# A planner's TensorE costs from measured spacings, another order of the projections, and buffers kept for the last heads

## The chip, the cores and the metric

The kernel runs on one core of a Trainium2 chip. The metric is the device time of one execution in microseconds (us), as the median of several runs. A core has TensorE (PE: matrix products and transposes, with its weight loads as PEld), VectorE (DVE), ScalarE (ACT), GpSimd (POOL) and SyncE (SP), which issues the DMAs here. Each engine takes its instructions in the order in which the program lists them, and waits for the results that an instruction needs.

## The reference

Two layers work on 512 tokens of width 1024. Each layer has one input projection whose columns feed three mixers side by side, one output projection, a norm, and an MLP with a hidden layer of 4096.

```python
for l in range(DEPTH):
    proj = h @ w_in[l]
    ...
    mixed = concatenate([nsa_mixer(nq, nkv, ngate, ...),      # 6 query heads, 2 kv heads
                         gla_mixer(gq, gk, gv, glr, gog, ...), # 6 heads, chunks of 64
                         pool_mixer(pu, pool_w[l], pool_scale[l])])
    h = layer_norm(ALPHA * h + mixed @ w_out[l], ln1_g[l], ln1_b[l])
    ff = square(relu(h @ w_up[l])) @ w_down[l]
    h = layer_norm(ALPHA * h + ff, ln2_g[l], ln2_b[l])
```

The attention mixer (`nsa_mixer`) rotates queries and keys (partial rotary embedding), and mixes three branches by gates: keys compressed from blocks of 32 tokens by a small two-layer network, selected blocks, and a window. The gated linear attention (`gla_mixer`) computes a masked product inside each chunk of 64 tokens, a running state over the chunks, a norm of each head and an output gate. All is float32.

## The kernel before

Float32 products are made of three products of parts: each operand is split into a rounded high part and a remainder (type float32r), ACT makes the high part and VectorE or GpSimd subtracts to get the low part. Weights arrive by DMA in units of up to 512 KB, in a fixed order, four raw units at a time; each unit is split the same way (`splits`, L342 on), and the unit's products may run when the split is done.

What sets the order on every engine is a planner (`class Planner`, L35 to L126), which runs while the program is built. Each piece of work is a generator, and has a priority; a `yield` ends a step and names what the next step waits for: events, a free PSUM bank (of 8), or a free slot among the NSLOT = 46 buffers of 128 x 512 floats. Whenever a piece of work is ready by the planner's own clock, its next step is emitted; when none is, a step of the background is, which is the weight products. The planner's clock is advanced by estimates: `MM` (L174) and `TR` (L180) carry those of TensorE, `act`, `tt`, `ts`, `stt`, `red` (L185 to L220) those of the others. `tt` with the engine "any" takes VectorE or GpSimd, by which of the two would end sooner by the estimates (L197 to L200).

The background of a layer runs through blocks in the order of the letters in `ORDER` (L1662): A values of the gated linear attention, B its queries and keys, D the first keys and values of the attention (K0, V0, K1: features as rows, 512 tokens as columns), E its other values and the gates (tokens as rows, 274 columns), F the keys K2, W the first layer of the network for compressed keys, G the queries, C the input of the trailing means, O the output gate, P and R those rows of the output projection that do not need the attention, N its other three rows. After that comes the MLP. Its first six tiles of rows of `w_up` are held in slots once they are split (`held`, L303 and L362) and used by `early_up` (L1317), each for the first 256 tokens as soon as those are normed, and for the others later; `out_rest` of tokens 256 to 511 stands between the first two tiles' products and the others'.

Around that background stand, as generators of their own:

- `states` (L697 on) and `intra` (L733 on), small products of the gated linear attention with 32 or 64 rows, `intra_mask` (L761, a mask on VectorE), and then for each tile of 128 tokens 28 small products or fewer with 64 columns and the states, and `rms` (L769);
- `rope` (L891): a shuffle on VectorE (L893) out of PSUM, two multiplications and a sum; K0 and V0 are then arranged by `im2col` (L955);
- `attention` (L1097), which starts one `head` (L1106) after another, first for tokens 0 to 255 (H = 0), six heads in two branches each, then for tokens 256 to 511 (H = 1). A head's products fill PSUM; VectorE takes the maximum, ACT the exponential, VectorE or another engine scales, TensorE transposes, ACT and VectorE split, TensorE multiplies with the values. The pair of heads 2m, 2m + 1 makes row m of the output projection's operand (`nmix`), by ACT, VectorE, ACT, VectorE.

Of the kernel before, what the change touches and what calls it, by code (L numbers as in the profile page):

```python
# [9 lines left out]
F32 = mybir.dt.float32  # L10
F32R = mybir.dt.float32r
# [23 lines left out]
class Planner:  # L35
    """Fixes the order in which each engine gets its instructions.

    A piece of work is a generator.  It emits instructions, and a yield ends a step: None waits for what the step
    has emitted, a list waits for conditions (names of events, or ("bank", n) for n free PSUM banks).  The matrix
    products of the projections are the background; they fill the tensor engine between the steps of the others.  # L40
    """
# [61 lines left out]
    def run(self):  # L103
        back_cond = None
        while self.work or self.back is not None:
            ready = [w for w in self.work if self.when(w[3]) <= self.now]
            if ready:
                w = min(ready, key=lambda w: w[:2])
                more, cond = self.step(w[2])
                if more:  # L110
                    w[3] = cond
                else:
                    self.work.remove(w)
                continue
            if self.back is not None and self.when(back_cond) <= self.now:
                more, cond = self.step(self.back)
                back_cond = cond if isinstance(cond, list) else None
                if not more:
                    self.back = None
                continue  # L120
            times = [self.when(w[3]) for w in self.work]
            if self.back is not None:
                times.append(self.when(back_cond))
            t = min(times)
            assert t < math.inf, ("nothing can go on", [w[3] for w in self.work], back_cond)
            self.now = max(self.now, t)  # L126
# [3 lines left out]
def trunk_kernel(ctx: ExitStack, tc, x, w_in, cmp_pos, cmp_w1, cmp_w2, gla_w_gate2, gla_b_gate,  # L130
# [12 lines left out]
    pl = Planner()  # L143
# [7 lines left out]
    def drop(n=1):  # L151
        """n slots have got their last reader"""
        pl.live -= n
# [20 lines left out]
    def MM(o, a, b, start, stop, loose=False):  # L174
        n = b.free_size()
        pl.pe(max(0.025, n / 2400.0 * (4 if b.dtype == F32 else 1) + 0.0025))
        nc.tensor.matmul(o, a, b, start=start, stop=stop, **({"skip_group_check": True} if loose else {}))  # L177
        pl.ready[o.tensor.name] = pl.now + 0.2

    def TR(o, a, i):  # L180
        pl.pe(0.056)
        nc.tensor.transpose(o, a, i)  # L182
        pl.ready[o.tensor.name] = pl.now + 0.2
# [157 lines left out]

    def splits():  # L342
# [14 lines left out]
        for i in range(len(units)):  # L357
# [4 lines left out]
            if i in held:  # L362
                yield [("raw", i), ("h", held[i] + 0.5, 0), ("slot", 1)]
                hi, lo = [slot(dt=F32R).rearrange("p (k n) -> p k n", k=kk) for _ in range(2)]
            else:
                yield [("raw", i)] + room(i)
                hi = wp.tile([128, kk, n], F32R, tag="whi", name=f"wh{i}", bufs=NSPL)
                lo = wp.tile([128, kk, n], F32R, tag="wlo", name=f"wl{i}", bufs=NSPL)
# [4 lines left out]
    def pair_sums(i0, i1, room, order):  # L373
        """operands of the seven products (Winograd's form of Strassen's) for two tiles of rows of the hidden layer"""
# [88 lines left out]
    def transpose_h(l, t, hT):  # L463
        """(l, t): tokens t of the input of layer l, or of its MLP for l + 0.5"""
# [50 lines left out]
    def passes(ps, sh, sl_, mh, ml, first, last, loose=False):  # L515
        """three products of parts: stationary (sh, sl_), moving (mh, ml)"""
# [35 lines left out]
    def layer_work(l, hT, nhT):  # L552
# [264 lines left out]
        def mixed(ks, t):  # L817
            """what the products with rows ks of w_out need for tile t"""
# [218 lines left out]
        def cmp_tile(t):  # L1037
            """probabilities of the compressed branch for one tile of queries"""
# [58 lines left out]
        def attention():  # L1097
            for H in range(2):
                for hh in range(6):
                    for br in (1, 2):  # L1100
# [3 lines left out]
                        pl.spawn(head(H, hh, br), 4)  # L1104

# [211 lines left out]
        def early_up(m, H, ffp, acc):  # L1317
            """rows m of the first part of the MLP's hidden layer, for half H of the tokens"""
# [24 lines left out]
        def token_sums():  # L1343
            """sums and differences of quarters (half of the rows, half of the tokens) of the MLP's input"""
# [43 lines left out]
        def up_pairs(up, ff):  # L1388
            """the hidden layer, two tiles of rows at a time; the last two products of a pair come among the next's"""
# [11 lines left out]
        def up_pair(i0, i1, ff, m):  # L1401
            """two tiles of rows of the hidden layer by seven products of quarters"""
# [259 lines left out]
ORDER = 'ABDEFWGCOPNR'  # L1662
# [59 lines left out]
```

## Time and profile before

| | |
|---|---|
| three runs | 1256.07, 1264.20, 1262.56 us (median 1262.56) |
| the profiled execution, its span | 1255.8 us |
| busy TensorE (PE) | 1232.5 us, 98%, 7377 products |
| busy VectorE (DVE) | 914.2 us, 73% |
| busy ScalarE (ACT) | 589.8 us, 47% |
| busy GpSimd (POOL) | 288.3 us, 23% |

The profiled execution's own time is its span; what lies around it is not in the profile, and the lowest of the runs is 0.3 us above it. Busy time of TensorE is modelled from the ends of products, so small gaps inside a run of products do not show as idle time; starts of products do show them. Layer 1 takes the first 630 us or so, and layer 2 repeats its stretches; times below are of layer 1.

### The profile page before, as it was taken

To read this page: it belongs to the slowest core of one execution; us is meant where nothing else is said; L and a number is where in the kernel's file an instruction comes from. 1 tells how busy PE (TensorE), PEld (TensorE's weight loads), DVE (VectorE), ACT (ScalarE), POOL (GpSimd) and SP (SyncE) were. 2 spreads that over 40 slices of the span, in tenths; PEclk is the share of its full clock that TensorE was granted. 3 is DMA by queue.
4 is the path that set the end of the run, shared out by engine and by line. 5 is a ranking of instruction groups with operands and counts; after the bars stand their busy time and mean duration, and the time that the engine had idled before them with its cause. 6 is when DMAs were issued, how large, how long until landed. Compare 5 with 4: busy or idle time off the path is not lost.

```text
span 1255.8 us, 19154 instructions
## 1 busy us (share of the span) xinstructions
PE 1232.5 (98%) x7377; PEld 1062.5 (85%) x7377; DVE 914.2 (73%) x1595; ACT 589.8 (47%) x1109; POOL 288.3 (23%) x302
## 2 busy tenths in 40 slices
PE   8999989999999999999999998999999999999997
PEld 7778878789989889899887787887898898998985
DVE  3768898888578477475657789988866874855856
ACT  4614457664336347255144245666643472562640
POOL 0135332124421010010121444311334300200202
PEclk9989999999999999999999999999999999999999
DMA  6412201235123333234153031021342242242331
GB/s 221 130 38 73 68 18 67 77 99 154 59 76 109 111 86 129 73 92 156 47 138 83 26 97 59 18 71 56 119 134 84 73 130 84 85 135 67 102 118 67
DMA packets 128523, 113.89 MB, mean 91 GB/s; under 512 B 17168, under 2 KB 103728, under 8 KB 128432
## 3 DMA queue, kind: packets, MB, share of 16 engines
q1 hardware_dynamic: 128432, 112.67, 29.3%
q8 instruction: 58, 0.95, 0.3%
q14 instruction: 33, 0.27, 0.1%
HBM read 110.56 MB, written 2.10 MB: 90 GB/s over the span
## 4 chain that ended last, share of the span: by engine, by line
PE 91%; DVE 7%; DMA 1%; issue 0%; ACT 0%; POOL 0%; SPq 0%; POOLq 0%; DVEq 0%
PE b L177 88%; PE b L182 3%; DVE s L202 2%; DVE s L215 2%; DVE nb L219 1%; DVE wl L202 1%; DMA h<-in_x_dram 1%; DVE f L227 0%; DVE s L208 0%; DVE den L208 0%; POOL s L202 0%; ACT s L190 0%; SPq L318 0%; DVE m L219 0%; DVE h L215 0%
## 5 line engine op out<-in xcount | busy, mean ns | idle before, releaser
L177 PE MATMUL b<-wh,s 128*128 128x512 f32 x1280 | 413.9, 397 | 0.4 <-ACT s L190 0.4
L202 DVE TENSOR_TENSOR wl<-wr,wh 128x1024 fp32r<-128x1024 f32 (+4 forms) x183 | 224.0, 1230 | 177.3 <-ACT wh L190 176.7
L190 ACT ACTIVATE wh<-wr 128x1024 fp32r<-128x1024 f32 (+4 forms) x194 | 184.4, 954 | 287.9 <-PE b L177 203.4
L177 PEld LDWEIGHTS b<-wh,s 128*128 128x128 f32 x1280 | 240.5, 188 | 54.9 <-ACT s L190 0.9
L177 PE MATMUL b<-wl,s 128*128 128x512 f32 x640 | 252.4, 394 | 0.0
L190 ACT ACTIVATE s<-s 128x512 fp32r<-128x512 f32 (+5 forms) x328 | 186.8, 586 | 78.5 <-DVE s L202 69.7
L177 PE MATMUL b<-s,s 128*128 128x256 f32 (+8 forms) x1360 | 214.7, 300 | 0.0
L177 PEld LDWEIGHTS b<-s,s 128*128 128x128 f32 (+4 forms) x1360 | 175.9, 188 | 25.0 <-issue 19.1
L190 ACT ACTIVATE s<-b 128x384 fp32r<-128x384 f32 (+9 forms) x228 | 105.3, 474 | 183.8 <-PE b L177 134.0
L177 PE MATMUL b<-hTh,wh 128*128 128x256 f32 (+1 forms) x544 | 178.2, 328 | 0.0
L177 PE MATMUL b<-hTh,wl 128*128 128x256 f32 (+1 forms) x544 | 175.9, 323 | 0.0
L177 PE MATMUL b<-hTl,wh 128*128 128x256 f32 (+1 forms) x544 | 175.8, 323 | 0.0
L202 DVE TENSOR_TENSOR s<-s,s 128x512 fp32r<-128x512 f32 (+5 forms) x192 | 145.2, 766 | 20.6 <-ACT s L190 17.7
L202 DVE TENSOR_TENSOR s<-b,s 128x256 f32<-128x256 f32 (+7 forms) x260 | 122.9, 481 | 47.5 <-PE b L177 39.3
L177 PEld LDWEIGHTS b<-wl,s 128*128 128x128 f32 x640 | 120.4, 188 | 26.5 <-POOL wl L202 0.7
L177 PEld LDWEIGHTS b<-hTh,wh 128*128 128x128 f32 x544 | 103.2, 190 | 11.2 <-issue 3.0
L202 POOL TENSOR_TENSOR s<-s,s 128x512 f32<-128x512 f32 (+5 forms) x52 | 68.8, 1324 | 189.3 <-DVE s L893 78.4
L202 POOL TENSOR_TENSOR s<-wr 128x512 f32<-128x512 f32 x24 | 37.0, 1543 | 322.8 <-DMA wr<-in_w_up_dram 282.9
L177 PEld LDWEIGHTS b<-hTh,wl 128*128 128x128 f32 x544 | 103.4, 190 | 8.9
L177 PE MATMUL b<-hTh,s 128*128 128x256 f32 x576 | 110.1, 284 | 0.0
L177 PEld LDWEIGHTS b<-hTl,wh 128*128 128x128 f32 x544 | 103.3, 190 | 7.8
L177 PEld LDWEIGHTS b<-hTh,s 128*128 128x128 f32 x576 | 92.1, 191 | 0.4
(140 smaller groups left out, 1602.2 us busy)
## 6 DMA issues: line engine op xcount, KB each, us to landing
wr<-in_w_down_dram SPq DMA_DIRECT2D x64, 512.0 KB, 3.8
wr<-in_w_up_dram SPq DMA_DIRECT2D x52, 512.0 KB, 4.0
wr<-in_w_out_dram SPq DMA_DIRECT2D x20, 512.0 KB, 3.5
wr<-in_w_in_dram SPq DMA_DIRECT2D x24, 384.0 KB, 3.1
wr<-in_w_up_dram SPq DMA_DIRECT2D x24, 256.0 KB, 3.1
wr<-in_w_in_dram SPq DMA_DIRECT2D x8, 400.0 KB, 3.2
wr<-in_w_in_dram SPq DMA_DIRECT2D x6, 512.0 KB, 3.6
h<-in_x_dram SPq DMA_DIRECT2D x4, 512.0 KB, 7.9
```

Source lines behind the costliest of these rows:

```text
L177: nc.tensor.matmul(o, a, b, start=start, stop=stop, **({"skip_group_check": True} if loose else {}))
L182: nc.tensor.transpose(o, a, i)
L190: nc.scalar.activation(o, a, func, scale=scale, **kw)
L202: e.tensor_tensor(out=o, in0=a, in1=b, op=op)
L215: nc.vector.scalar_tensor_tensor(o, a, s, b, op0=op0, op1=op1)
L219: nc.vector.tensor_reduce(o, a, axis=AX.X, op=op, negate=negate)
```

## The change

Three things change, and nothing else that reaches the chip: the estimates in `MM` and `TR`, the string `ORDER` (E before D, and G before W), and a further condition for splitting the held units of `w_up`: two free slots instead of one, and either that the last head has been started (the new event `heads`) or that eight slots are free.

```diff
     def MM(o, a, b, start, stop, loose=False):
         n = b.free_size()
-        pl.pe(max(0.025, n / 2400.0 * (4 if b.dtype == F32 else 1) + 0.0025))
+        if b.dtype == F32R:
+            pl.pe(max(0.109, 0.006 + 0.4414e-3 * n))
+        elif b.dtype == F32:
+            pl.pe(2 * max(0.112, 0.99e-3 * n))
+        else:
+            pl.pe(max(0.038, 0.0025 + 0.4167e-3 * n))
...
     def TR(o, a, i):
-        pl.pe(0.056)
+        pl.pe(0.109)
...
+    def spare(l):
+
+        return 0.0 if (l, "heads") in pl.events or pl.live + 8 <= NSLOT else math.inf
...
             if i in held:
-                yield [("raw", i), ("h", held[i] + 0.5, 0), ("slot", 1)]
+                yield [("raw", i), ("h", held[i] + 0.5, 0), ("slot", 2), lambda: spare(held[i])]
...
                         pl.spawn(head(H, hh, br), 4)
+            ev("heads")
...
-ORDER = 'ABDEFWGCOPNR'
+ORDER = 'ABEDFGWCOPNR'
```

Comments and docstrings also go, which shifts line numbers: what is L177 before is L182 after, L182 is L187, L202 is L207. The same operations are issued in all, but some that may go to either engine change it: GpSimd has 223 `tensor_tensor` instead of 257, VectorE 1037 instead of 1007 and six `tensor_scalar` more, ACT two activations fewer.

The order on TensorE, at the place where D ends and E begins, before; `b_533` is the PSUM bank of K1, `b_760` takes a masked product of a chunk, `b_766` values:

```order
L177 MATMUL b_533<-hTl_118,wh_542 128x512
L177 MATMUL b_533<-hTh_117,wl_543 128x512
L177 MATMUL b_760<-s_525,s_526 128x128 x4
L177 MATMUL b_766<-wh_588,hTh_117 128x274
L177 MATMUL b_766<-wl_589,hTh_117 128x274
L177 MATMUL b_766<-wh_588,hTl_118 128x274
```

And after, where E (`b_735`) ends and D (`b_775`, K0) begins, with the first products on masked chunks (`b_791`) behind it:

```order
L182 MATMUL b_735<-wh_461,hTh_117 128x274
L182 MATMUL b_735<-wl_462,hTh_117 128x274
L182 MATMUL b_735<-wh_461,hTl_118 128x274
L182 MATMUL b_775<-hTh_117,wh_493 128x512
L182 MATMUL b_775<-hTl_118,wh_493 128x512
...
L182 MATMUL b_791<-s_257,s_647 128x64
L182 MATMUL b_791<-s_257,s_676 128x64
```

All of E and the products on masked chunks now stand ahead of the rest of D; before, they stood behind it.

The order on VectorE around the first rotation of a key (the shuffle out of the bank of K0), before; `cf` holds masks, `dec` the decay of the states:

```order
L202 TENSOR_TENSOR wl_704<-wr_540,wh_703 128x1024
L893 STREAM_SHUFFLE s_723<-b_531 128x512
L202 TENSOR_TENSOR s_724<-b_531,s_119 128x512
L202 TENSOR_TENSOR s_728<-b_706,cf 128x512
L202 TENSOR_TENSOR s_735<-b_663,cf 128x256
L202 TENSOR_TENSOR s_735<-b_663,cf 64x128
L215 SCALAR_TENSOR_TENSOR s_735<-s_711,dec_553,s_735 128x256
L215 SCALAR_TENSOR_TENSOR s_735<-s_711,dec_557,s_735 64x128
L202 TENSOR_TENSOR s_750<-b_730,cf 128x512
L893 STREAM_SHUFFLE s_752<-b_533 128x512
```

And after; `r` are the factors of the norm of a chunk's heads, `wl` low parts of weights:

```order
L207 TENSOR_TENSOR s_843<-b_810,r_858 128x384
L224 TENSOR_REDUCE r_884<-s_873 128x6
L207 TENSOR_TENSOR s_860<-b_830,r_871 128x384
L207 TENSOR_TENSOR wl_893<-wr_544,wh_892 128x1024
L207 TENSOR_TENSOR s_873<-b_845,r_884 128x384
L207 TENSOR_TENSOR wl_921<-wr_593,wh_920 128x768
L207 TENSOR_TENSOR wl_946<-wr_800,wh_945 128x768
L902 STREAM_SHUFFLE s_955<-b_775 128x512
L207 TENSOR_TENSOR s_956<-b_775,s_119 128x512
L902 STREAM_SHUFFLE s_971<-b_777 128x512
```

The masks, the states and the norms of all four tiles now stand ahead of the first rotation; before, they stood among and behind the rotations.

The order on TensorE at the end of the attention, where the last head's product with compressed values (`vcs`) is followed by the output projection of tokens 256 on; before, with 48 products of `early_up` (`b_3040`) between, of which the last two stand here:

```order
L177 MATMUL b_3009<-s_1875,vcs_133 128x256
...
L177 MATMUL b_3040<-hTl_2441,s_3006 128x256
L177 MATMUL b_3040<-hTh_2440,s_3007 128x256
L177 MATMUL b_3110<-wh_3023,s_2550 128x512
...
L177 MATMUL b_3110<-wh_3073,s_3090 128x512
```

And after:

```order
L182 MATMUL b_3056<-s_1804,vcs_133 128x256
L182 MATMUL b_3120<-wh_2938,s_2534 128x512
...
L182 MATMUL b_3120<-wh_2997,s_2849 128x512
...
L182 MATMUL b_3120<-wh_3026,s_3149 128x512
```

The products of `early_up` now stand among the last heads, and six products of the output projection between the last head and the first product that needs it (the last row here: `s_3090` before, `s_3149` after).

## Rows read from the trace of the kernel before

**Rows 1.** The page: span, and the chain that ended last by engine.

```profile
span 1255.8 us, 19154 instructions
...
PE 91%; DVE 7%; DMA 1%; issue 0%; ACT 0%; POOL 0%; SPq 0%; POOLq 0%; DVEq 0%
```

**Rows 2.** Busy time by stretch: length, PE, PEld, DVE, ACT, POOL, PEclk, DMA share, GB/s.

```profile
62.50:69.40 6.90, 6.90 (x17) 3.81 (x16) 4.28 (x11) 0.00 (x0) 0.00 (x0) 0.51 0.20 57
78.37:199.50 121.13, 116.33 (x707) 97.76 (x706) 110.51 (x262) 59.35 (x153) 53.36 (x73) 1.00 0.17 52
133.15:192.30 59.15, 54.47 (x336) 47.02 (x335) 56.29 (x146) 31.90 (x96) 23.71 (x36) 1.00 0.10 32
```

**Rows 3.** Timeline of PE, 82 to 103 us: start, length, engine, line, operation.

```profile
82.38 0.39 PE L177 MATMUL b<-hTl,wh 128*128 128x512 f32 x1
82.61 0.40 PE L177 MATMUL b<-hTh,wl 128*128 128x512 f32 x1
82.94 1.15 PE L177 MATMUL b<-s,s 32*128 32x128 f32 x8
84.02 0.40 PE L177 MATMUL b<-wh,hTh 128*128 128x274 f32 x1
...
90.23 12.44 PE L177 MATMUL b<-s,s 128*128 128x64 f32 x76
102.60 0.39 PE L177 MATMUL b<-wh,hTh 128*128 128x274 f32 x1
```

**Rows 4.** DVE by form, 78.37 to 199.5: busy us, mean ns | idle before.

```profile
L202 DVE TENSOR_TENSOR wl<-wr,wh 128x768 fp32r<-128x768 f32 x7 | 8.5, 1232 | 2.1 <-ACT wh L190 2.1
L202 DVE TENSOR_TENSOR wl<-wr,wh 128x1024 fp32r<-128x1024 f32 x6 | 7.5, 1255 | 6.3 <-ACT wh L190 6.3
...
L202 DVE TENSOR_TENSOR s<-b,r 128x384 f32<-128x384 f32 x4 | 2.1, 552 | 0.0
...
L202 DVE TENSOR_TENSOR s<-b,cf 128x512 f32<-128x512 f32 x3 | 2.0, 682 | 0.0
L219 DVE TENSOR_REDUCE r<-s 128x6 f32<-128x384 f32 x4 | 2.0, 545 | 0.0
...
L202 DVE TENSOR_TENSOR s<-b,s 64x256 f32<-64x256 f32 x4 | 1.7, 415 | 0.1
...
L215 DVE SCALAR_TENSOR_TENSOR s<-s,dec,s 64x128 f32<-64x128 f32 x3 | 1.4, 469 | 0.0
L215 DVE SCALAR_TENSOR_TENSOR s<-s,dec,s 128x256 f32<-128x256 f32 x3 | 1.4, 466 | 0.0
...
L202 DVE TENSOR_TENSOR s<-b,cf 128x256 f32<-128x256 f32 x3 | 1.2, 412 | 0.0
...
L202 DVE TENSOR_TENSOR s<-b,cf 64x128 f32<-64x128 f32 x3 | 0.8, 272 | 0.0
```

**Rows 5.** Timeline of PE, 59 to 68 us.

```profile
59.86 6.17 PE L177 MATMUL b<-s,s 32*128 32x128 f32 x28
...
66.97 0.63 PE L177 MATMUL b<-hTh,wl 128*128 128x512 f32 x1
67.40 0.63 PE L177 MATMUL b<-hTh,wh 128*128 128x512 f32 x1
```

**Rows 6.** Timeline of DVE and POOL, 137 to 141 us.

```profile
137.22 3.00 POOL L202 TENSOR_TENSOR s<-s,s 128x512 f32<-128x512 f32 x2 [1.89 <-DVE s L893]
137.63 3.14 DVE L202 TENSOR_TENSOR s<-s,s 128x512 f32<-128x512 f32 x2
```

**Rows 7.** Timeline of PE, ACT and DVE, 272 to 279 us.

```profile
272.81 0.49 PE L177 MATMUL b<-s,vcs 32*128 32x256 f32 x2
...
274.66 0.38 ACT L190 ACTIVATE s<-b 64x256 f32<-64x256 f32 x1
...
277.27 0.40 ACT L190 ACTIVATE s<-s 128x256 fp32r<-128x256 f32 x1
...
278.54 0.42 DVE L202 TENSOR_TENSOR s<-s,s 128x256 fp32r<-128x256 f32 x1
```

More of the change, by code (lines that the diff above doesn't have):

```diff
@@ L124, in run @@
             t = min(times)
-            assert t < math.inf, ("nothing can go on", [w[3] for w in self.work], back_cond)
+            assert t < math.inf, ("nothing can go on", self.now, self.live, len(self.banks), [(w[2].gi_code.co_name, w[3]) for w in self.work], back_cond)
             self.now = max(self.now, t)
```

## Prediction

> **What bounds the kernel now.** I read the page first. TensorE is busy for 98% of the span and holds 91% of the chain that ended last; VectorE holds 7%; the span is 1255.8 us [rows 1]. So a change of order can give back only what TensorE loses, and can cost whatever TensorE is newly made to wait for. The change alters no product, so I looked for the stretches where TensorE loses time, by busy time per stretch [rows 2]. From the first rotation of a key on VectorE (78.37 us) to VectorE's last piece for the sixth head of the first half (199.50 us) the stretch lasts 121.13 us, TensorE is busy for 116.33 of them and VectorE for 110.51. TensorE stands still there for 121.13 - 116.33 = 4.8 us, and layer 2 repeats that. In its second part, 133.15 to 192.30, VectorE works 56.29 of 59.15 us, 95%: there VectorE, not TensorE, is the engine without slack. The other loss is the clock: from 62.50 to 69.40 us TensorE was granted 0.51, its lower level of 1.2 GHz [rows 2]. The stretches of the MLP are left out, since there only costs of the planner change and no block moves.
>
> **The change, part by part.** No instruction is added or taken away; what is counted below is who stands beside whom.
>
> *Values before keys.* The value projection E (two weight units of 48 products each) now runs before the key projection D. In the trace of before the first half of E runs from 84.02 to 90.23 us, after D's keys were done [rows 3]: 6.2 us, twice that with the second half, 12.4 us. With it the products of masked chunks, 90.23 to 102.60 us, 12.4 us, and two groups of eight small ones like that at 82.94 (to 84.02, 1.1 us each, 2.2 us) now come before the keys. So of the work that TensorE had between the first key rotation and the last head of the first half, 12.4 + 12.4 + 2.2 = 27.0 us go ahead of it. The stretch would shrink from 121.13 to 94.1 us if TensorE alone decided, and those 27.0 us are paid earlier.
>
> VectorE does not lose as much from this stretch. What goes ahead with those products is, by [rows 4]: the norms of the chunks (2.1 + 2.0 us), the low parts of the values (1.7), three masks (2.0), the states (1.2 + 0.8 + 1.4 + 1.4), and four of the seven weight splits of 768 columns (4 x 1.23 = 4.9). Sum: 18.9 us. What comes in: one more weight split of 1024 columns (1.25 us) and four operations of 512 columns that GpSimd did before (0.7 each, 2.8 us), 4.0 us with the few small ones that cancel. VectorE then has 110.5 - 18.9 + 4.0 = 95.6 us of work in a stretch in which TensorE has 94.1, and TensorE cannot end it sooner than VectorE does, because the last heads' transposes read what VectorE's queue delivers last. Bounds: if VectorE is never idle the stretch is 95.6 us, 1.5 over what moving alone gives; if it is busy for 91% as over the whole stretch now (110.51 of 121.13), it is 95.6/0.912 = 104.8, 10.7 over. The nearest row is the crowded second part with 95%: 95.6/0.952 = 100.4, 6.3 over. Part of the idle time is for weights that ACT has yet to round (6.3 and 2.1 us before the two kinds of splits [rows 4]); fewer such splits are left, so I take the value between the first bound and the nearest row, **+4 us** per layer.
>
> *Fewer changes between large and small products.* Before, four groups of small products stand alone among D's large ones between 68 and 84 us. Each costs a longer step in (82.61 to 82.94, 0.33 us, where 82.38 to 82.61 is 0.23) and, by my estimate, as much out [rows 3], so about 0.2 us. Now they stand in two solid runs. Four to ten changes fewer: -0.8 to -2.0 us, I take **-1.2 us** per layer.
>
> *The clock.* 28 small products of 32 or 64 rows fill 59.86 to 66.0 us, the clock falls among them, and the large products after them still take 0.43 us each (66.97 to 67.40) instead of 0.23 [rows 3, 5]. Now two solid runs of small products follow each other, with twelve products of E (1.5 us at 6.2 for 48) between; the second holds two states (eight products) and three groups like the one at 82.94, some 5 us at the higher level. If the clock falls and rises as it does now, nothing changes. If it stays at 1.2 GHz through the second run, at half the rate that costs up to 5 us more. The nearest row is the clock as it is now, so I take **+0.7 us** per layer, near the lower end.
>
> *Buffers kept for the last heads.* Before, 48 products of the MLP's first rows stand between the last head's product (272.81 us) and the output projection, 5.8 us. They hide the chain ACT, VectorE, ACT, VectorE that turns that head into an operand, from 274.66 to 278.96 us (VectorE's two steps are alike) [rows 7]. Now these 48 and others of their kind are spread among the last heads, and only six large products (1.4 us) are left between the last head and the product that needs it. The bare chain is 0.38 + 0.42 + 0.40 + 0.42 = 1.6 us and three hops; as it ran it ended 278.96 - 273.30 = 5.7 us after. So the new wait lies between 0.2 and 4.3 us. The row as it ran was lengthened by three weight splits that stood ahead on VectorE; in the new order three to five shorter ones do. I take **+1.5 us** per layer.
>
> *The planner's costs* (0.232 for a 512-column product instead of 0.216, 0.109 for a transpose instead of 0.056) issue nothing. They make the planner put other work a little earlier among TensorE's. Queries before compressed keys puts 72 products (16.7 us at 0.23) ahead of the compressed keys' first layer; VectorE's work for both lies inside the stretch above and is counted there. Both at nothing of their own. The cover is that stretch; if it does not hold, the price is the 10.7 us above.
>
> Sum per layer: 4 - 1.2 + 0.7 + 1.5 = +5.0 us, +10 us for both. The profiled execution took 1255.8 us, at the low end of the three runs (1256.07 lowest, median 1262.56, 0.5% above). From 1255.8 I get **1266 us**; what the runs scatter upward is not added. Its own range: lower ends, 1.5 - 2.0 + 0 + 0.2 = -0.3 per layer, 1255; all upper ends seldom come together (10.7 - 0.8 + 5 + 4.3 = 19.2 per layer); half way to them gives 1275.
>
> **Rivals.** *VectorE gets faster (about 1243 us).* GpSimd loses 34 element-wise operations to VectorE over both layers. Where both work, both slow: two 512-column operations took 3.14 us on VectorE while GpSimd had two of its own, against 0.68 for one in the mean of another form of that size [rows 4, 6]. If the stretch on VectorE loses a tenth by this, it takes 86 us, TensorE decides (94.1) and its 4.8 us of waits go as well: -4.8 - 1.2 = -6.0 per layer, 1255.8 - 12 = 1244, and with a shorter chain at the end 1243. It decides from 86/94 on. The Trainium skill, page "SBUF — State Buffer", section "Who interferes with whom", states this as a rule: an operation of VectorE with two SBUF inputs and one of GpSimd that reads SBUF block each other for a whole instruction. By that rule the trace's 3.14 us agree, and fewer operations on GpSimd would free VectorE. Against it: GpSimd keeps 223 of 257 such operations, and the ones that move cost VectorE their own time. Chance 0.17.
>
> *VectorE's queue is held by late weights (about 1278 us).* In VectorE's fixed order three splits of weights now stand directly ahead of the first key rotation, and others among the rotations. Each waits for ACT to have rounded its weight; that idle time was 6.3 + 2.1 = 8.4 us [rows 4] while VectorE had slack, and it stood beside TensorE's long runs. If all of it remains, the stretch is 95.6 + 8.4 = 104.0, 9.9 over, and the layer 9.9 - 1.2 + 0.7 + 1.5 = +10.9: 1255.8 + 22 = 1278. It crosses the 1% mark if about 8 us per layer of the 8.4 remain, or 6 with the clock's upper half. For it: the keys' work now begins with no reserve. Chance 0.29.
>
> *Nothing comes of it (1250 to 1258 us).* If VectorE's new work fits into waits that are there anyway (the 4.8 us are partly for GpSimd's and ACT's results, not VectorE's), and the last chain into TensorE's own lag, the layer comes out within 2 us of now. Chance 0.14.
>
> **How the numbers follow.** My forecast has 0.40. What a measurement of this kernel tells from no change is about 1%, 12.6 us: 1249.9 to 1275.2. The first rival is faster (0.17); the second lies beyond 1275.2 (0.29); my forecast and the third rival lie between (0.54). The range for 8 in 10 reaches into both rivals: from 1246, which takes in the upper part of the first, to 1284, six above the second's value, for 3 us per layer of a longer run at the lower clock.
>
> **What would show it.** In the changed profile: (1) the stretch from the first key rotation to the last head of the first half near 98 us, with VectorE busy for 95% or more; at 94 or less the first term is wrong, at 104 the second rival is right. (2) Waits of TensorE on VectorE's operands among the first heads that are longer than now, and on ACT's scaled heads. (3) The granted clock: one stretch at half near 60 us of about 7 us, or a longer one. (4) A wait of TensorE of 1 to 2 us at the third product of the output projection's last rows. (5) No change in the MLP's stretches. I am wrong altogether if TensorE is idle less than now in the attention part, or if time appears in the MLP.

## The result and the profile after

The changed kernel took 1307.34 us (median of four runs, 1305.41 to 1310.10), the kernel before 1263.38 beside it: ratio 1.0352 [1.0312, 1.0392], 44 us slower. The forecast was 1266 us in 1246 to 1284: wrong, 23 us above the upper end. It added 10 us to the 1255.8 of one profiled execution; the change is measured against a median that is 7.6 us above that, and adds 44.

The page of the changed kernel, span, engines and chain, answers to [rows 1]:

```profile
span 1304.0 us, 19137 instructions
...
PE 1254.2 (96%) x7377; PEld 1085.4 (83%) x7377; DVE 924.5 (71%) x1631; ACT 590.0 (45%) x1107; POOL 259.0 (20%) x268
...
PE 79%; DVE 15%; DMA 2%; issue 2%; SPq 1%; ACT 1%; DVEq 0%; POOLq 0%; POOL 0%; ACTq 0%
```

Two things are to be seen. VectorE's share of the chain doubled, from 7 to 15%, while it has hardly more work (924.5 us for 914.2). And the same 7377 products keep TensorE busy 21.7 us longer (1254.2 - 1232.5), while it stands still for 49.8 us (1304.0 - 1254.2) where it was 23.3. So of the 48.2 us between the two spans 26.5 are waits and 21.7 are products that took longer, at the lower clock (granted 0.97 over the whole span after, 0.99 before).

Where they lie: busy time by stretch of the changed kernel, cut at the first key's rotation, at VectorE's last piece for the sixth head of the first half, at the first product of the output projection that needs the last head, and at the same product near the end of layer 1's MLP (columns as in [rows 2]); and below it the stretches of the kernel before that were not shown.

```profile
0.00:113.34 113.34, 107.80 (x538) 85.45 (x539) 51.21 (x106) 39.26 (x68) 13.54 (x18) 0.89 0.36 107
113.34:219.61 106.27, 93.57 (x508) 81.13 (x507) 101.25 (x234) 56.03 (x141) 47.52 (x58) 0.92 0.17 53
219.61:305.65 86.04, 82.41 (x495) 67.14 (x493) 74.14 (x143) 52.77 (x117) 16.05 (x21) 1.00 0.29 87
305.65:651.10 345.45, 344.17 (x2147) 308.70 (x2148) 228.40 (x328) 148.14 (x232) 48.18 (x35) 1.00 0.31 97
651.10:1304.00 652.90, 626.24 (x3696) 543.00 (x3694) 469.52 (x826) 293.81 (x552) 133.71 (x136) 0.97 0.28 84
```

```profile
0.00:78.37 78.37, 74.64 (x347) 56.32 (x348) 39.73 (x73) 33.86 (x54) 7.76 (x10) 0.96 0.49 146
199.50:280.48 80.98, 80.75 (x488) 66.65 (x487) 68.65 (x135) 52.47 (x116) 15.54 (x21) 1.00 0.26 81
280.48:623.90 343.42, 343.42 (x2148) 308.67 (x2147) 230.69 (x321) 150.02 (x236) 62.64 (x45) 1.00 0.33 101
623.90:1255.80 631.90, 617.38 (x3696) 533.11 (x3694) 464.59 (x808) 294.08 (x553) 148.96 (x153) 0.99 0.28 87
```

| layer 1, us | before | after | difference | forecast |
|---|---|---|---|---|
| to the first key's rotation | 78.37 | 113.34 | +35.0 | +26.5 (27.0 - 1.2 + 0.7) |
| to the sixth head | 121.13 | 106.27 | -14.9 | -23.0 (4 - 27.0) |
| to the output projection | 80.98 | 86.04 | +5.1 | +1.5 |
| sum | 280.48 | 305.65 | +25.2 | +5.0 |

The stretch behind it, up to the same product, takes 345.45 us where it took 343.42. These 2.0 us come in its first 22 us, with a wait of 0.47 us in the output projection (shown below) and one of 0.80 us at 325.46 for a normed tile; from 330 us on the changed kernel stays 27.2 us behind to the end of layer 1, so the MLP itself is as long as before. What is left, layer 2, repeats the loss: 631.90 us before, 652.90 after. Layer 1's 25.2, these 2.0 and layer 2's 21.0 make the 48.2. In the middle stretch VectorE is busy for 101.25 of 106.27 us, 95%; TensorE stands still for 12.7 us there, where it was 4.8 [rows 2], and was granted 0.92.

What TensorE waited for in the whole run of the changed kernel (total us, times, longest us):

```profile
PE b L182 <- DVE s L220: 10.9, 2, 5.5
PE b L182 <- DVE s L207: 9.6, 8, 3.0
PE b L182 <- DVE wl L207: 8.7, 3, 3.7
PE b L182 <- ACT s L195: 3.3, 2, 1.7
PE b L187 <- DMA posr<-in_cmp_pos_dram: 2.2, 1, 2.2
```

The longest, with TensorE's timeline behind it (last column: idle before, and what ended it):

```profile
158.45 0.69 PE L182 MATMUL b<-s,s 128*128 128x128 f32 x2 [5.44 <-DVE s L220]
...
161.93 0.63 PE L182 MATMUL b<-hTh,wl 128*128 128x512 f32 x1
162.35 0.63 PE L182 MATMUL b<-hTh,wh 128*128 128x512 f32 x1
```

A head's first product waits 5.44 us for the low part of a rotated query, and the 512-column products behind it start 0.42 us apart, not 0.23 as in [rows 3]. So part of that wait is paid again in clock: from 158.45 to 165.00 us TensorE was granted 0.51, its lower level of 1.2 GHz.

```profile
158.45:165.00 6.55, 6.55 (x26) 5.69 (x26) 6.28 (x11) 1.17 (x5) 2.29 (x1) 0.51 0.58 212
```

What VectorE did meanwhile, with GpSimd's operation beside it:

```profile
153.22 2.83 DVE L207 TENSOR_TENSOR wl<-wr,wh 128x1024 fp32r<-128x1024 f32 x1
...
157.71 0.69 DVE L220 SCALAR_TENSOR_TENSOR s<-s,s 64x512 fp32r<-64x512 f32 x1
158.43 0.96 DVE L207 TENSOR_TENSOR wl<-wr,wh 128x768 fp32r<-128x768 f32 x1
```

```profile
152.71 2.25 POOL L207 TENSOR_TENSOR wl<-wr,wh 128x768 fp32r<-128x768 f32 x1
```

VectorE is nowhere idle for more than 0.1 us between these rows. A weight split stands in its queue ahead of the pieces that TensorE waits for, and takes 2.83 us while GpSimd works too, against 1.255 counted [rows 4]. VectorE's two kinds of splits in the middle stretch, by form (as in [rows 4]):

```profile
L207 DVE TENSOR_TENSOR wl<-wr,wh 128x1024 fp32r<-128x1024 f32 x6 | 10.6, 1769 | 0.1
...
L207 DVE TENSOR_TENSOR wl<-wr,wh 128x768 fp32r<-128x768 f32 x4 | 4.2, 1044 | 3.3 <-ACT wh L195 3.2
```

The tail of the attention, TensorE's timeline at the output projection:

```profile
305.65 0.51 PE L182 MATMUL b<-wh,s 128*128 128x512 f32 x1 [1.65 <-ACT s L195]
305.99 0.40 PE L182 MATMUL b<-wl,s 128*128 128x512 f32 x1
306.86 0.73 PE L182 MATMUL b<-wh,s 128*128 128x512 f32 x2 [0.47 <-DVE s L207]
```

### The profile page after: what moved, and what is told of

The parts are those of the page before. It is cut to its first block, busy times and chain, and to the rows that moved or that the text cites. A ratio compares the mean times of both kernels' runs of the same rounds, so it can differ in the third digit from the quotient of the medians.

```text
span 1304.0 us, 19137 instructions
## 1 busy us (share of the span) xinstructions
PE 1254.2 (96%) x7377; PEld 1085.4 (83%) x7377; DVE 924.5 (71%) x1631; ACT 590.0 (45%) x1107; POOL 259.0 (20%) x268
## 4 chain that ended last, share of the span: by engine, by line
PE 79%; DVE 15%; DMA 2%; issue 2%; SPq 1%; ACT 1%; DVEq 0%; POOLq 0%; POOL 0%; ACTq 0%
PE b L182 77%; DVE s L207 6%; PE b L187 3%; DVE wl L207 2%; DVE h L220 2%; DVE s L220 1%; DMA wr<-in_w_in_dram 1%; SPq L323 1%; DMA wr<-in_w_up_dram 1%; DVE nb L224 1%; DVE s L902 0%; ACT s L195 0%; DVE h L207 0%; DVE hTl L207 0%; ACT wh L195 0%
## 5 line engine op out<-in xcount | busy, mean ns | idle before, releaser
L182 PE MATMUL b<-wh,s 128*128 128x512 f32 x1280 | 415.3, 398 | 4.3 <-ACT s L195 3.3
L207 DVE TENSOR_TENSOR wl<-wr,wh 128x1024 fp32r<-128x1024 f32 (+4 forms) x179 | 222.3, 1244 | 168.8 <-ACT wh L195 168.2
L182 PEld LDWEIGHTS b<-wh,s 128*128 128x128 f32 x1280 | 240.3, 188 | 60.4 <-ACT s L195 4.2
L182 PE MATMUL b<-wl,s 128*128 128x512 f32 x640 | 252.3, 394 | 0.0
L195 ACT ACTIVATE s<-s 128x512 fp32r<-128x512 f32 (+6 forms) x328 | 187.2, 587 | 124.7 <-DVE s L207 120.9
L182 PE MATMUL b<-s,s 128*128 128x256 f32 (+8 forms) x1360 | 220.1, 306 | 18.7 <-DVE s L220 10.9
L182 PEld LDWEIGHTS b<-s,s 128*128 128x128 f32 (+4 forms) x1360 | 180.6, 193 | 42.1 <-issue 15.9
L195 ACT ACTIVATE s<-b 128x384 fp32r<-128x384 f32 (+8 forms) x228 | 105.7, 472 | 183.9 <-PE b L182 147.4
L182 PE MATMUL b<-hTh,wh 128*128 128x256 f32 (+1 forms) x544 | 177.7, 327 | 0.0
L182 PE MATMUL b<-hTh,wl 128*128 128x256 f32 (+1 forms) x544 | 175.9, 323 | 0.0
L182 PE MATMUL b<-hTl,wh 128*128 128x256 f32 (+1 forms) x544 | 175.8, 323 | 0.0
L207 DVE TENSOR_TENSOR s<-b,s 128x256 f32<-128x256 f32 (+6 forms) x260 | 122.3, 481 | 73.6 <-PE b L182 49.0
L207 DVE TENSOR_TENSOR s<-s,s 128x512 fp32r<-128x512 f32 (+4 forms) x204 | 146.0, 724 | 17.2 <-ACT s L195 13.5
L182 PEld LDWEIGHTS b<-wl,s 128*128 128x128 f32 x640 | 120.4, 188 | 25.7
L182 PEld LDWEIGHTS b<-hTh,wh 128*128 128x128 f32 x544 | 103.8, 191 | 10.1 <-issue 2.0
L182 PE MATMUL b<-hTh,s 128*128 128x256 f32 x576 | 110.9, 284 | 0.0
L182 PEld LDWEIGHTS b<-hTh,wl 128*128 128x128 f32 x544 | 103.4, 190 | 8.8
L182 PEld LDWEIGHTS b<-hTl,wh 128*128 128x128 f32 x544 | 103.5, 190 | 8.2
L207 POOL TENSOR_TENSOR s<-wr 128x512 f32<-128x512 f32 x24 | 34.6, 1442 | 355.4 <-DMA wr<-in_w_up_dram 334.5
L182 PEld LDWEIGHTS b<-hTh,s 128*128 128x128 f32 x576 | 92.3, 191 | 0.1
L182 PE MATMUL b<-hTl,s 128*128 128x256 f32 x288 | 81.4, 283 | 0.0
```

The costliest lines, as they stand in the source:

```text
L195: nc.scalar.activation(o, a, func, scale=scale, **kw)
L207: e.tensor_tensor(out=o, in0=a, in1=b, op=op)
```

## The experiments

Ratios are to the kernel before in the same comparison, with 95% intervals. Letters in the expectations: A, VectorE has more to do than fits (load); B, not the amount but where single results stand in the orders (place); C, the planner's estimates are out of proportion to each other.

### The parts apart and together

First `order_alone`, the new `ORDER` with the old costs:

```diff
-ORDER = 'ABDEFWGCOPNR'
+ORDER = 'ABEDFGWCOPNR'
```

> The kernel before with only the order of the projections changed (values before keys, queries before compressed keys); the planner's costs as before. Theory A: keys that come late leave VectorE more work than TensorE has between the first key rotation and the heads; the order alone then brings most of the 44 us: 1290 to 1310 us, with a stretch from first key rotation to the sixth head of about 106 us, and VectorE busy over 95% of it. Theory B: the new TensorE costs do it, since they place work so that it meets operands that are not ready; then the order alone costs 0 to 10 us: 1255 to 1275.

Then `costs_alone`: `MM`, `TR` and the condition for the held buffers as in the change, `ORDER` as before.

> The changed kernel with the old order of the projections: the new TensorE costs, and the held buffers' condition, without which the planner finds no way on. Theory A: within 8 us of before, 1255 to 1272, with TensorE's waits among the first heads as before (5 to 8 us a layer). Theory B: 1285 to 1310.

With the old costs, one swap each, `values_first_alone` and `queries_first_alone`:

```diff
-ORDER = 'ABDEFWGCOPNR'
+ORDER = 'ABEDFWGCOPNR'   # values_first_alone
+ORDER = 'ABDEFGWCOPNR'   # queries_first_alone
```

> The kernel before with only the values (E) ahead of the keys (D). Theory A: this swap carries the loss: 1285 to 1305; counting VectorE's work against TensorE's from the first key rotation on, VectorE has 13 to 14 us a layer more up to the last of the first heads, twice that is 27, and a longer run at the lower clock adds up to 8. Theory B: 1255 to 1275.

> The kernel before with only the queries (G) ahead of the compressed keys' first layer (W). Theory A: VectorE's work never runs ahead of TensorE's here, so within 6 us of before: 1256 to 1268. A rival to A: the rotations of the queries crowd VectorE just where the heads begin, and this swap carries the loss, 1280 or more.

And the whole change less one swap, `without_values_first` and `without_queries_first`:

```diff
-ORDER = 'ABEDFGWCOPNR'
+ORDER = 'ABDEFGWCOPNR'   # without_values_first
+ORDER = 'ABEDFWGCOPNR'   # without_queries_first
```

> The changed kernel with the values behind the keys again (new costs, queries ahead of compressed keys). If the swap of values and keys carries the loss even here: 1265 to 1285. If the parts' losses do not add because each one uses the same slack of VectorE: 1290 to 1305, about as much as the new costs alone.

> The changed kernel with the compressed keys' first layer ahead of the queries again (new costs, values ahead of keys). The compressed keys' products then meet operands that VectorE has not made, as with the values-first order alone (waits of 7.3 and 4.8 us a layer there): 1305 to 1320, slower than the changed kernel, in which the queries' 16.7 us of products stand in between.

Measured, with the change itself (medians: order alone 1319.51 us, costs alone 1302.55, values first 1309.30, queries first 1293.56, without values first 1288.63, without queries first 1341.32). Costs alone came out as theory B said and queries alone as its rival said; the others lie outside the ranges given, `without_queries_first` by 21 us:

| | old order | E before D | G before W | both |
|---|---|---|---|---|
| old costs | 1 | 1.0354 [1.0327, 1.0381] | 1.0229 [1.0197, 1.0260] | 1.0435 [1.0403, 1.0467] |
| new costs | 1.0273 [1.0216, 1.0329] | 1.0614 [1.0585, 1.0644] | 1.0188 [1.0145, 1.0230] | 1.0352 [1.0312, 1.0392] |

Every kernel but the old one is slower. Values before keys costs something in every pair of columns: 3.5% alone, 3.4 on the new costs, 2.1 on queries first, 1.6 on both. The other two behave differently: the new costs take 2.7% alone and 2.6 where only the values stand first, but where queries stand first they take nothing that can be told from zero (-0.4) or give 0.8 back; queries first takes 2.3% alone and 0.8 behind values first, and gives 0.9 and 2.6 back on the new costs. So no part has a price of its own. From `without_values_first` the change divides into 1.9% (24 us) for costs and queries, and 1.6% (20 us) for the values.

The condition on held buffers has no column, because it moves nothing: the program with it alone lists every engine's instructions as before, and the change lists them the same without it. Only on new costs with the old order does the planner need it to get to an end.

What the single parts lose is not one wait. With the values first (old costs) it is the operands of the compressed keys that are late; TensorE's timeline of `values_first_alone`:

```profile
126.52 0.55 PE L177 MATMUL b<-s,wh 128*128 128x248 f32 x1 [7.10 <-DVE s L202]
...
132.96 0.57 PE L177 MATMUL b<-s,wh 128*128 128x248 f32 x1 [4.50 <-DVE s L202]
...
136.92 0.58 PE L177 MATMUL b<-s,wh 128*128 128x248 f32 x1 [1.99 <-POOL s L202]
```

Queries before W put other products between, but with the old costs this does not take the wait away; TensorE's timeline of `order_alone`:

```profile
144.90 0.58 PE L177 MATMUL b<-s,wh 128*128 128x248 f32 x1 [7.14 <-DVE s L202]
```

With the new costs the change has one wait of 3.74 us left at these products, for a weight's low part (`wl`), where `without_queries_first` has waits of 3.18 and 4.85 us and shorter ones for their operands. With the costs alone the longest waits are in the tail; TensorE's timeline of `costs_alone`:

```profile
295.74 1.75 PE L187 MATMUL b<-ident,s 128*128 128x128 f32 x7 [2.64 <-DVE s L213]
...
302.10 0.80 PE L182 MATMUL b<-wh,s 128*128 128x512 f32 x1 [1.37 <-ACT s L195]
```

### VectorE's load

`after_less_dve` and `before_less_dve` keep every engine's other orders and let ACT do VectorE's splits of the blocks' weights, as a scaled copy:

```diff
-        e.tensor_tensor(out=o, in0=a, in1=b, op=op)
+        if relief and eng == "dve":
+            nc.scalar.activation(o, a, AF.Copy, scale=1e-4)
+        else:
+            e.tensor_tensor(out=o, in0=a, in1=b, op=op)
```

> The changed kernel with every engine's order kept, but 16 weight splits per layer (from the keys' weights to the output projection's) leave VectorE: their low part is written by ACT as a scaled copy, so the output is not the reference's. Theory A (VectorE has no slack from the first key rotation on, and sets TensorE's pace): 16 operations of about 1.1 us, some 17 us a layer, leave it; the stretch from the first key rotation to the last of the first heads falls from 106.8 us to 95 to 98 us, where TensorE's own 94 us hold, and the waits of 3.9 and 5.6 us before the first heads shorten to under half; 1270 to 1285 in all. Theory B (TensorE waits for chains of single results, not for a full queue): 1298 or more.

> The same on the kernel before: the same 16 or so splits per layer go to ACT, orders kept, so the output is not the reference's. Theory A: VectorE has more idle time here, so the gain is at most half of that on the changed kernel: 1248 to 1262. Theory B: no gain or a loss, as ACT is loaded more: 1260 to 1275.

On the changed kernel 1.0247 [1.0220, 1.0273], 1294.57 us: 1.05% back, 13 us. On the kernel before 0.9992 [0.9970, 1.0014], nothing. So the load is real and it is the change that made it matter, but 13 us is less than load alone was to give: 1294.57 lies between the ranges of the two theories. The wait of 3.7 us for `wl` is gone and the longest one shrank from 5.5 to 3.6, not to under half; waits of `after_less_dve`:

```profile
PE b L182 <- DVE s L210: 8.6, 8, 2.7
PE b L182 <- DVE s L223: 7.2, 2, 3.6
PE b L182 <- ACT s L195: 3.3, 2, 1.7
```

So more was taken off: in `after_front_lean` also VectorE's sums and low parts of `im2col`; in `after_tail_lean` only the splits that fall into the tail (N's second unit, the first held rows of `w_up`); in `after_lean` both, and in `before_lean` both on the kernel before.

```diff
-                               OP.add, "any")
+                               OP.add, "any", relief=True)
...
+        relieved.update(u["N2"])
+        relieved.update(i for p in u["M"][0][0] for i in p)
```

> The changed kernel, all orders kept; VectorE loses the 16 weight splits a layer that the lean run before took away and also its share of arranging the compressed blocks (sums with positions and low parts, some 13 operations a layer), all written by ACT as scaled copies, so that part of the computation is left out. If a full queue on VectorE sets the pace up to the heads, another 6 to 9 us a layer go: 1278 to 1285. If what is left (3.8 and 2.8 us a layer) are chains of single results: 1291 to 1296, as with the splits alone.

> The changed kernel, all orders kept; only VectorE's splits near the end of the attention (the output projection's last rows, and the held first rows of the MLP, some 13 a layer, 8 to 9 us) go to ACT as scaled copies. VectorE was busy 9.9 of every 10 us there. If it sets the pace, the waits of TensorE there (6.5 us a layer over the kernel before) fall by 4 to 6 us: 1295 to 1300. If the last heads' own chains do: 1303 to 1309.

> Both of these at once on the changed kernel. VectorE as the cause of the whole loss: 1263 to 1278, near the kernel before. Otherwise the waits that are left show what else: 1285 or more.

> Both on the kernel before. With the splits alone it did not move (ratio 0.999). If VectorE does not bound it: 1255 to 1266. If it gains as much as the changed kernel, the changed kernel's loss is not VectorE's: 1240 or less.

Measured: 1.0188 [1.0160, 1.0216]; 1.0340 [1.0301, 1.0378]; 1.0154 [1.0126, 1.0183]; and on the kernel before 1.0013 [0.9987, 1.0039]. In front the load costs 20 us (1.0352 to 1.0188), in the tail nothing that can be told from zero, together 25, by the intervals some 6 either way. The first and the third of these times lie between the ranges given for them; the other two say that VectorE bounds neither the tail nor the kernel before.

The middle stretch shows the load directly. Between the same two products, at the first key's rotation and at the sixth head's end, it lasted in the change, in `after_less_dve`, in `after_lean` and (last row, cut the same way in the old order) in `before_lean`:

```profile
113.46:219.84 106.38, 93.68 (x508) 81.23 (x507) 101.36 (x233) 56.23 (x142) 47.52 (x58) 0.92 0.17 53
113.25:212.06 98.81, 92.36 (x508) 79.80 (x506) 91.71 (x226) 62.46 (x149) 44.38 (x58) 0.93 0.19 57
112.56:207.99 95.43, 89.54 (x507) 77.05 (x506) 79.80 (x202) 71.51 (x173) 44.80 (x58) 0.96 0.20 59
83.53:204.72 121.19, 116.37 (x708) 97.82 (x707) 85.88 (x227) 77.33 (x187) 53.33 (x73) 1.00 0.17 52
```

As VectorE's work falls from 101.36 to 79.80 us the stretch falls by 11.0, to 95.43; layer 2 shows the same (106.42 to 95.43). On the kernel before VectorE's work fell from 110.51 to 85.88 and the stretch did not move (121.13 and 121.19). What was taken off includes splits that ran long beside GpSimd; amount and crowding are not told apart here.

The pages of `after_lean` and, behind it, `before_lean`:

```profile
span 1281.2 us, 19083 instructions
...
PE 1247.6 (97%) x7377; PEld 1078.2 (84%) x7377; DVE 837.1 (65%) x1525; ACT 651.1 (51%) x1213; POOL 252.6 (20%) x268
```

```profile
span 1266.1 us, 19109 instructions
...
PE 1242.5 (98%) x7377; PEld 1067.0 (84%) x7377; DVE 832.7 (66%) x1491; ACT 649.9 (51%) x1213; POOL 288.6 (23%) x302
```

With the load away on both, 15.1 us remain between the spans: TensorE stands still 10.0 us longer (33.6 and 23.6) and is busy 5.1 us longer. Cut by products, and set against the 27.0 us moved per layer, 9.8 of the 15.1 lie in the two tails (86.18 us in layer 1, where `before_lean` has 81.22), 3.1 ahead of the first key's rotations and 2.4 in the middle stretches, and the rest is 0.2 shorter. What it still waits for in `after_lean` among the first heads and in the tail is one head's operand and single results of ACT, and `posr` (see below) in layer 1:

```profile
PE b L182 <- DVE s L210: 9.2, 6, 3.5
PE b L182 <- ACT s L195: 4.0, 2, 2.0
PE b L187 <- DMA posr<-in_cmp_pos_dram: 1.9, 1, 1.9
```

### Two single waits

`posr_first` issues the two loads of `posr` (the position table of the compressed keys) ahead of the block before.

```diff
+            pv_ = cmp_pos[l].rearrange("a r d -> (a r) d")
+            dma(posr[:, 0:64], pv_)
+            dma(posr[:, 64:128], pv_)
...
-            pv_ = cmp_pos[l].rearrange("a r d -> (a r) d")
-            dma(posr[:, 0:64], pv_)
-            dma(posr[:, 64:128], pv_)
```

> The changed kernel with two small loads (posr, positions of the compressed blocks) issued ahead of the other small parameters; the order on TensorE and VectorE is the same. TensorE waited 2.2 us for them at 28 us in layer 1 only, and for some 1.5 us more right behind. If that wait is lost time, it vanishes and the kernel gains 2.5 to 4 us: 1303 to 1305; if the time is lost elsewhere anyway, 1306 to 1309.

1.0347 [1.0306, 1.0389]. The wait at 28.22 us is gone, and one of 1.62 us for a weight's low part stands at 32.78 instead; the interval cannot tell the 3 us in question. Inconclusive.

`tail_cover` puts the 48 products of `early_up` behind the start of the last head again, so that they hide its chain as they did before:

```diff
+            if (H, hh) == (1, 5):
+                ev("lasthead")
...
+                    yield [E("lasthead")]
```

> The changed kernel in which the first rows of the MLP's hidden layer wait for the last head's product, so that all 48 products stand between it and the output projection again, as in the kernel before. If they were missing as cover there, the waits of 1.8 and 0.6 us at the output projection and some of the waits of 0.5 to 1.1 us among the last heads go: 8 to 13 us less over two layers, 1294 to 1300. If the last heads then wait for their own results instead, for want of those products among them: 1304 to 1310.

1.0418 [1.0388, 1.0448], 1315.14 us: 8 us slower than the change, and above both ranges. The wait at the output projection is gone, and the heads themselves stand uncovered; TensorE's timeline of `tail_cover`:

```profile
292.19 0.56 PE L182 MATMUL b<-s,s 128*128 128x256 f32 x3 [0.79 <-DVE s L207]
...
298.19 0.56 PE L182 MATMUL b<-s,s 128*128 128x256 f32 x3 [3.07 <-DVE s L207]
```

There is one cover for two places.

### The planner's proportions

If the new costs lose because only TensorE's became longer, lengthening the others' should heal them. In the planner's helper for VectorE, ACT and GpSimd, `costs_all_scaled` on `costs_alone` by 1.08, and `changed_others_raised` on the change by 1.15:

```diff
-        end = start + cost
+        end = start + 1.08 * cost   # costs_all_scaled; 1.15 in changed_others_raised
```

> The new TensorE costs with the old order of the projections (as in the run of the costs alone), and all estimates of VectorE, ACT and GpSimd raised by 8%, as much as a 512-column product's was. Theory C: the old costs kept TensorE, VectorE and ACT in proportion, all too short, and the new ones broke it, so that TensorE's consumers are placed too early; raising the others brings most back: 1266 to 1282. Rival: what counts is where the last products of the MLP's first rows stand, and the small products' doubled estimate, which the 8% do not touch: 1292 to 1308.

> The changed kernel with all estimates of VectorE, ACT and GpSimd raised by 15%. Theory C: consumers are placed later, the waits before the first heads (3.9, 5.6 and 3.2 us a layer) shrink by half: 1285 to 1297. If VectorE has no slack there, no order of TensorE helps and the time stays: 1300 to 1312.

1.0189 [1.0158, 1.0220] where `costs_alone` has 1.0273, so 11 us of its 35 by the ratios; but 1.0690 [1.0644, 1.0735] for the change, 43 us worse. The first time, 1286.67 us, lies between its two ranges, the second, 1347.24, far above both. So raising the other estimates is no remedy. Each factor also makes another order, so the 11 us do not show that proportion as such matters, and why the new costs alone lose stays open.

## Why the prediction was wrong

**The step that failed first is "Values before keys", +4 us per layer.** The limit it named was right: VectorE ends the stretch, busy for 95%, as point (1) of the list said. Its size was not. The stretch was to last 98.1 us and lasted 106.27, 12.2 over what moving alone gives (94.1). Taking VectorE's load off brought 11.0 of these back, so the mechanism is shown and the term was mis-sized. Three things were behind it:

- The sum of what leaves VectorE is wrong: the terms listed make 17.5 us, not 18.9. With it VectorE has 97.0 us of work, not 95.6, and the bounds become 2.9 and 12.3 over, not 1.5 and 10.7; the measured 12.2 lies just under the upper one. The value chosen was near the lower.
- VectorE's work was counted at its old durations, and was 101.25 us. The six wide splits alone took 3.1 us more, at 1769 ns instead of 1255. Three of them lasted 1.64 to 2.83 us, each beside an operation of GpSimd; two others beside one took 1.23 and 1.38.
- A stretch in which VectorE is full costs TensorE more than the waits: of the 12.2, 7.9 are standing still (12.7 - 4.8), the other 4.3 are longer products, at a granted clock of 0.92 instead of 1.00. With VectorE's load off, TensorE's busy time there fell from 93.68 to 89.54 us.

The Trainium skill, page "TensorE: Matmul & The Clock Gate", section "Part 1: The HAM clock gate", says that throttled is the default state of TensorE's clock and that activity releases it. The trace agrees: behind the wait of 5.44 us TensorE was at its lower level, at 0.42 us a product.

**"27.0 us paid earlier"** cost 35.0, where 26.5 was forecast with "fewer changes" and "the clock". TensorE is busy there for 33.2 us more (107.80 - 74.64) and stands still 1.8 longer (5.54 - 3.73, with the wait for `posr`, 2.2 us, which layer 2 does not have). In layer 2 the stretch grew by 29.4, from 74.37 us (623.90 to 698.27) to 103.77 (651.10 to 754.87). What is above 27.0 is mostly clock. The change is at half in two stretches, around both runs of small products:

```profile
66.00:76.00 10.00, 10.00 (x30) 5.90 (x28) 0.61 (x2) 0.00 (x0) 0.00 (x0) 0.50 0.01 2
79.70:86.40 6.70, 6.70 (x32) 6.48 (x31) 5.11 (x12) 0.84 (x1) 0.00 (x0) 0.50 0.00 0
```

The kernel before was at half from 62.50 to 69.40 us in its profiled execution, and longer in others (see the last section): in `before_less_dve`, with the same order on TensorE, the first key's rotation begins at 82.63 us instead of 78.36. Set against that execution the stretch grew by 30.7 us in layer 1 and by 25.6 in layer 2 (78.21 us there). So the moved work was sized rightly, and how far the clock's term was off depends on the execution of before that one takes; the forecast took a lucky one.

**"Queries before compressed keys ... both at nothing of their own"**, with the planner's costs, was the second error, and of the same weight: 24 us of the 44 are there without the values' swap. The reason given was that they issue nothing and that their work lies inside the stretch counted above. But they reorder what TensorE meets, and each alone costs 2.3 to 2.7%; which single waits make up these times was not taken apart.

**"Buffers kept"**: the wait came at the named place and in the named size, 1.65 + 0.47 us for +1.5 (bounds 0.2 to 4.3), point (4). Its cause was wrong: the condition on buffers moves nothing; costs and order scatter the 48 products. The whole tail costs 5.1 us, since the transposes and products of the last heads wait as well, and `tail_cover` shows that giving the cover back to the end takes it from them. Behind the tail another 2.0 us (1.6 in layer 2) were not forecast; with VectorE's splits of the tail on ACT they are gone (304.95 to 648.50 us in `after_tail_lean`, 343.55).

**The rivals.** VectorE did not get faster with fewer operations on GpSimd: a split took 2.83 us beside one of GpSimd's. The rule of the Trainium skill ("SBUF — State Buffer", "Who interferes with whom"), that an operation of VectorE with two SBUF inputs and one of GpSimd that reads SBUF block each other, agrees with that row. What I took from it was wrong: GpSimd kept 268 instructions, and in the middle stretch it is as busy as before (47.52 of 106.27 us, 45%; before 53.36 of 121.13, 44%). The rival of VectorE's queue named the right place and the wrong mechanism: by the list, 104 us or more in that stretch was to prove it right, but idle time for weights that ACT has yet to round was 3.4 us before the two kinds of splits, less than the 8.4 of before; VectorE was not held, it was full. Its 1278 us was the nearest figure, by luck. (By its own sum it crosses the 1% mark at 7.2 us per layer, 5.4 with the clock's upper half, not 8 and 6.) Points (2) and (3) came out as listed: longer waits on VectorE among the first heads, and a longer time at half clock. Point (5) held for the MLP itself, not for the 2.0 us ahead of it.

**What stays open.** Of the 44 us, 25 (22 of them seen in the middle stretch) are VectorE's load, shown by taking it off. The other 19 are, by the traces, about 5 per layer in the tail, in waits for single results, and the rest mostly ahead of the first key's rotation, in the clock, which scatters between executions, and in `posr` once. No experiment took these away without making another, so their shares are read, not shown.

## What to carry to other kernels

An order that a planner has fitted cannot be costed part by part: each of three harmless-looking edits cost 2 to 4% alone, 8.6% in sum, and 3.5% together. When work is moved out of a stretch, ask which engine is left there without slack, count its work at crowded durations, and count each wait of TensorE of a few microseconds with the slower products behind it. New estimates for one engine, though taken from measured spacings, can make a planner's order worse (here by 2.7%) when the other engines' estimates, and the order that was tuned to them, stay as they were.

## What the runs showed of the hardware

The clock at one place differs between executions of the same TensorE order. From 62.50 us on, the kernel before (first row shown in [rows 2]) was granted its full clock of 2.4 GHz again at 69.40, but `before_less_dve`, whose TensorE order is the same, stayed at the lower level of 1.2 GHz; TensorE worked without a pause in both. Busy time by stretch, the kernel before and then `before_less_dve`:

```profile
69.40:76.00 6.60, 6.60 (x28) 3.86 (x27) 1.27 (x4) 0.00 (x0) 0.00 (x0) 1.00 0.01 2
```

```profile
62.50:69.40 6.90, 6.90 (x17) 3.66 (x16) 4.50 (x12) 0.00 (x0) 0.00 (x0) 0.50 0.21 57
69.40:76.00 6.60, 6.60 (x16) 2.96 (x15) 1.27 (x4) 0.00 (x0) 0.00 (x0) 0.50 0.00 0
```

In the same 6.60 us one issued 28 products and the other 16. The kernel before itself scatters like this: 13 runs in one comparison took 1256.96 us at a granted clock of 0.992 to 1266.86 at 0.984. A forecast made from one profile takes its luck for the kernel's own: the span of before is 1255.8 us, and with VectorE's load lowered, which changes no time that can be measured, 1265.8.
